# A bidirectional encoder block on one core: split V weights made anew in each group, chunks loaded in place and normalised four at a time, mixed tiles stored from ScalarE's queue

## The chip, the cores and the metric

The kernel runs on one core of a Trainium2 chip. The time is device microseconds of one execution. The kernel before took 1433.19 us, the median of three runs (1433.07, 1433.19, 1435.83). The engines are called TensorE (PE in the profile; PEld is its weight load), VectorE (DVE), ScalarE (ACT), GpSimd (POOL) and SyncE (SP, which here only issues transfers).

## What is computed

One layer on 2048 positions of 1024 features, in float32:

```
h = rms_norm(x, norm_g)
a_val, a_gate, g_conv, u, v, g_sgu = split(h @ w_in, 6)         # each 1024 wide
c = depthwise_conv(a_val * sigmoid(a_gate), width 31) + conv_b
y_conv = silu(layer_norm(c)) * silu(g_conv)
v = layer_norm(v)                                               # over 1024 features
mixed[head] = w_s[head] @ v[chunk of 128 positions, head] + b_s  # 8 heads, 16 chunks
y_sgu = u * mixed * silu(g_sgu)
out = rms_norm(x + concat(y_conv, y_sgu) @ w_out, final_g)
```

## The kernel before

**Numbers.** A float32 product is made of three matmuls in a rounded format: each operand is split into a high and a low part (`split`, L126: ScalarE copies the high part, VectorE subtracts it), and high x high, low x high and high x low are added up in PSUM. So every operand has an "h" and an "l" tile.

**Groups.** The positions are worked on in two groups (g = 0, 1) of two blocks (b = 0, 1) of 512. Each group has a V stage and then 20 units.

*V stage.* `v_mm` (four times 96 matmuls) projects a block onto one half of V's columns. Half 0 of both blocks comes first: `v0_done` takes the statistics of each chunk of 128 positions and stores the chunk to DRAM (`v_sp`). With half 1, `v1_done` (L268 to L281) loads the stored half again (`v0r`, L269), completes the chunk's statistics on VectorE and GpSimd, and normalises both halves on ScalarE (L278, L279) into a place that `room` gives: an r tile, two t tiles, or a w tile. `mix` then multiplies a chunk with the mixing matrices of its heads: two times four small matmuls (L224), a copy by ScalarE (`mixt`, L226) and a store (`mix_sp`, L227). Four chunks are mixed from hooks inside the last `v_mm`, four from the first unit's steps. `make_addend` (g = 0 only) sums the mixing matrices' rows on TensorE (`rsum`) and adds b_s (`bst`).

*The V weights.* `v_weights` (L180) loads them raw in the first group (`vraw`), splits them and stores the split tiles (`op_sp`, from GpSimd's queue, L190 and L191); in the second group it loads the split tiles.

*Sums and units.* `sums_of_a` makes four sums S1 to S4 of the blocks' operands (the `s` tiles, r tiles to s tiles by `split`), one slab of 128 features at a time. A unit makes 2 x 2 blocks of the projection from seven products (`product`, 12 matmuls each, L338) instead of eight, from operands `a` or `s` and weights `op`. The first group builds these weights from raw ones (`w`), a sum and a split each, and stores them to `op_sp`; the second loads them (L298). Some stand in a large tile called `ex`, most in w tiles.

*Conv.* After each conv unit `conv` (44 VectorE instructions) is put in with the lowest priority: a filler. The layer norm of the conv (`conv_ln`) runs later, as a generator in steps, between the output projections (`pa` for the SGU half, `po` for the conv half), which `ln_late` and `ln_first` advance.

**What sets the order.** The code gives each instruction a priority in program order (the conv a low one), and a scheduler at build time picks on each engine among those whose inputs would be there. Every engine then runs its list in that order, and waits at the head of it. Transfers too start in the order of the queue that issues them. A tile waits until its pool has a free buffer: 8 w tiles (512 KB), 3 r tiles (512 KB), 8 t tiles (256 KB), 8 large ones, 6 PSUM banks, and 2 more of these for mixing and small sums.

Of the kernel before, what the change touches and what calls it, by code (L numbers as in the profile page):

```python
# [8 lines left out]
F32 = mybir.dt.float32  # L9
# [5 lines left out]
P = 128  # L15
# [16 lines left out]
def hybrid_block(ctx: ExitStack, tc: tile.TileContext, xt, x, w, wo, wst, vecs, cw, bs, fg, out):  # L32
# [32 lines left out]

    op_sp = dram.tile([156, P, 1024], F32R, name="op_sp")
    v_sp = dram.tile([8, P, SG], F32, name="v_sp")
# [111 lines left out]

    def v_weights(g, half):  # L180
        tiles = []
        for kp in range(4):
            hi, lo = wtile("vh"), wtile("vl")
            at = 140 + half * 8 + kp * 2
            if g == 0:
                r = rtile("vraw")
                for u in range(2):
                    nc.sync.dma_start(r[:, u * 512:(u + 1) * 512], w[2 * half + u, :, kp * 512:(kp + 1) * 512])
# [30 lines left out]
    def mix(ch, zc, wsv):  # L219
        for half in range(2):  # L220
            px = xtile("mixp")
            for h in range(4):
                hd = half * 4 + h
                nc.tensor.matmul(px[:, h * P:(h + 1) * P], zc[half][:, h * P:(h + 1) * P], wsv[half][:, h * P:(h + 1) * P], start=True, stop=True)  # L224
            t = ttile("mixt")
            nc.scalar.activation(t, px, AF.Copy)  # L226
            nc.sync.dma_start(mix_sp[half * 4:half * 4 + 4, :, ch * P:(ch + 1) * P].rearrange("h d s -> d h s"),  # L227
                              t.rearrange("p (h q) -> p h q", h=4))

    def make_addend(wsv):  # L230
        for half in range(2):
            rp = xtile("rsum")
            nc.tensor.matmul(rp, ones, wsv[half], start=True, stop=True)
            bst = ttile("bst")
            nc.sync.dma_start(bst, bs[half * SG:(half + 1) * SG].partition_broadcast(P))
            for h in range(4):
                hd = half * 4 + h
                o = slice(h * P, (h + 1) * P)
                nc.vector.scalar_tensor_tensor(bst[:, o], rp[:, o], sln_b[:, hd:hd + 1], bst[:, o], mul, add)
            nc.sync.dma_start(ad_sp[:, half * 4:half * 4 + 4, :], bst.rearrange("p (h q) -> p h q", h=4))  # L240

    def v_dones(g, wsv):
# [9 lines left out]
        def v0_done_scaled(c, pv):  # L252
# [3 lines left out]
            nc.gpsimd.dma_start(v_sp[c], t)  # L256

        def room(c):
            if c < 3:
                z = rtile("z")  # L260
            elif c == 3:
                return [ttile("z"), ttile("z")]
            else:
                z = wtile("z").bitcast(F32)
            return [z[:, :SG], z[:, SG:]]

        def v1_done(c, pv):
            v0 = ttile("v0r")  # L268
            nc.sync.dma_start(v0, v_sp[c])  # L269
            nc.vector.bn_stats(stats[:, c, 1, :], pv)  # L270
            mv = small.tile([P, 4], F32, tag="mv", name="mv")
            nc.vector.bn_aggr(mv[:, 0:2], stats[:, c].rearrange("p a b -> p (a b)"))
            rs, nm = mv[:, 2:3], mv[:, 3:4]
            nc.gpsimd.tensor_scalar(mv[:, 1:2], mv[:, 1:2], EPS, None, add)
            rsqrt_small(rs, mv[:, 1:2])
            nc.gpsimd.tensor_scalar(nm, mv[:, 0:1], rs, -1.0, mul, mul)
# [8 lines left out]
        return v0_done, v0_done_scaled, v1_done, mix_next  # L285

# [239 lines left out]
    for j in range(2):  # L526
        X[0, j] = btile([P, 2, 4, SG], F32R, f"xg{j}")
    vw = v_weights(0, 0)
    vtiles = None
# [41 lines left out]
    def group(g, A, vtiles):  # L571
        wsv = mixing_weights()
        v0_done, v0_done_scaled, v1_done, mix_next = v_dones(g, wsv)
        if g == 0:
# [9 lines left out]
        v_mm(A, 1, 0, vtiles, v0_done)  # L584
        for t1 in v_weights(g, 1):
# [23 lines left out]
        def build():  # L609
            at = made[0]  # L610
            if at >= len(builders):
                return
            made[0] += 1
            gen, n, j = builders[at]
            if at % 12 < 8:
                t = wtile(f"op{n}_{j}")
            else:
                if ex[0] is None:
                    ex[0] = btile([P, 4, 1024], F32R, "ex")
                t = ex[0][:, at % 12 - 8, :]  # L620
# [11 lines left out]
        for n, (kind, i) in enumerate(units):  # L632
            steps = unit_steps(g, ops, tiles_of.setdefault(n, []), make[kind](i))
            for j in range(6):
                next(steps)
                if n == 0 and j < 4:
                    mix_next()
                    build()
                    if j > 1:
                        build()  # L640
# [16 lines left out]
                if g == 0 and n == NU - 1 and j == 3:  # L657
                    nv = None
                    for nv in v_weights(1, 0):
                        pass  # L660
                    staged_h(nextA, 3, rb[3])
# [88 lines left out]
    for ti in range(HEAD, NT):  # L750
# [16 lines left out]
        ln_first(ti - 12)  # L767

# [18 lines left out]
    for ti in range(NT):  # L787
# [4 lines left out]
        if ti < NT - 1:  # L792
            out_mm(po, yc[ti], 0, (0, 1), False)
            ln_late(ti + 4)
            out_mm(po, yc[ti], 1, (0, 1), True)
            ln_first(ti + 4)
        else:
# [61 lines left out]
```

## Time and profile before

| | |
|---|---|
| median of three runs | 1433.19 us |
| profiled execution, its own time | 1436.89 us |
| its span | 1435.1 us |
| TensorE busy | 1354.6 us, 94% |
| VectorE busy | 1125.2 us, 78% |
| ScalarE busy | 574.7 us, 40% |
| GpSimd busy | 228.9 us, 16% |
| moved by DMA | 341.72 MB, mean 238 GB/s |

All numbers of the trace come from the profiled execution. Busy time counts computing instructions only. The profile also divides the span into 40 slices of 35.9 us; TensorE's busy share in tenths and its granted clock in tenths of full speed read

```profile
PE   6897999999999999947999999999999999999996
PEclk9898999999999999977999999999999999999998
DMA  9326998798989995429877777777588653565641
```

A slice with a 9 is one in which TensorE worked for 90% of the time or more. The low digits lie at the start (first group's V stage), in slices 17 to 19 (second group's V stage and what follows) and at the end.

### The profile page before, as it was taken

To read this page: it belongs to the slowest core of one execution; us is meant where nothing else is said; L and a number is where in the kernel's file an instruction comes from. 1 tells how busy PE (TensorE), PEld (TensorE's weight loads), DVE (VectorE), ACT (ScalarE), POOL (GpSimd) and SP (SyncE) were. 2 spreads that over 40 slices of the span, in tenths; PEclk is the share of its full clock that TensorE was granted. 3 is DMA by queue.
4 is the path that set the end of the run, shared out by engine and by line. 5 is a ranking of instruction groups with operands and counts; after the bars stand their busy time and mean duration, and the time that the engine had idled before them with its cause. 6 is when DMAs were issued, how large, how long until landed. Compare 5 with 4: busy or idle time off the path is not lost. (4 is left out here: it accounts for less than half of the span.)

```text
span 1435.1 us, 17757 instructions
## 1 busy us (share of the span) xinstructions
PE 1354.6 (94%) x6044; PEld 1119.0 (78%) x6044; DVE 1125.2 (78%) x1771; ACT 574.7 (40%) x977; POOL 228.9 (16%) x438
## 2 busy tenths in 40 slices
PE   6897999999999999947999999999999999999996
PEld 5685877888888888836888888888878888788875
DVE  5875578999999999898989999998984112777772
ACT  5444434454445432233222322321244332666662
POOL 1221222333332311131101110110000000011110
PEclk9898999999999999977999999999999999999998
DMA  9326998798989995429877777777588653565641
GB/s 345 130 102 201 342 336 284 261 353 285 320 291 350 330 351 195 158 90 300 283 267 263 260 255 266 272 266 257 195 276 277 185 153 106 183 198 159 191 134 50
DMA packets 169754, 341.72 MB, mean 238 GB/s; under 512 B 15296, under 2 KB 84928, under 8 KB 169664
## 3 DMA queue, kind: packets, MB, share of 16 engines
q1 hardware_dynamic: 135936, 221.04, 47.4%
q0 software_dynamic: 33728, 119.56, 23.0%
q8 instruction: 47, 0.77, 0.2%
q14 instruction: 43, 0.35, 0.1%
HBM read 195.31 MB, written 145.23 MB: 237 GB/s over the span
## 5 line engine op out<-in xcount | busy, mean ns | idle before, releaser
L460 DVE SCALAR_TENSOR_TENSOR ca<-cx,cwt,ca 128x505 f32<-128x505 f32 (+1 forms) x240 | 180.8, 753 | 2.6 <-DMA op<-op_sp 1.4
L462 DVE SCALAR_TENSOR_TENSOR cb<-cx,cwt,cb 128x504 f32<-128x504 f32 (+1 forms) x224 | 168.0, 750 | 4.6 <-ACT cb L456 1.2
L468 DVE SCALAR_TENSOR_TENSOR cb<-cq,cws,cb 128x504 f32<-128x504 f32 (+1 forms) x224 | 168.1, 750 | 0.8
L338 PE MATMUL x<-s,op 128*128 128x512 f32 x648 | 156.2, 389 | 0.0
L338 PEld LDWEIGHTS x<-s,op 128*128 128x128 f32 x648 | 121.5, 188 | 25.1
L204 PE MATMUL v<-vh,a 128*128 128x512 f32 x448 | 123.3, 396 | 4.7 <-ACT a L128 2.4
L204 PEld LDWEIGHTS v<-vh,a 128*128 128x128 f32 x448 | 85.3, 191 | 24.7 <-ACT a L128 4.0
L338 PE MATMUL x<-a,op 128*128 128x512 f32 x336 | 86.7, 396 | 0.0
L338 PE MATMUL v<-a,op 128*128 128x512 f32 x336 | 83.5, 398 | 3.1 <-DVE t L425 3.1
L128 ACT ACTIVATE op<-w 128x512 fp32r<-128x512 f32 x96 | 57.6, 624 | 62.2 <-DVE w L314 41.9
L338 PE MATMUL z<-s,op 128*128 128x512 f32 x336 | 81.4, 391 | 0.0
L338 PE MATMUL y<-a,op 128*128 128x512 f32 x336 | 80.7, 389 | 0.0
L129 DVE TENSOR_TENSOR yl<-ys,yh 128x1024 fp32r<-128x1024 f32 x16 | 19.6, 1224 | 75.5 <-PE pa L684 64.7
L338 PEld LDWEIGHTS v<-a,op 128*128 128x128 f32 x336 | 64.5, 193 | 17.5 <-DVE t L425 3.9
L338 PE MATMUL v<-s,op 128*128 128x512 f32 x312 | 75.3, 390 | 1.6 <-ACT v L418 1.6
L338 PE MATMUL x<-s,ex 128*128 128x512 f32 x312 | 75.3, 389 | 0.0
L311 POOL DMA_DIRECT2D op_sp<-op x96 | 51.4, 535 | 149.6 <-DVE op L129 140.2
L338 PEld LDWEIGHTS x<-a,op 128*128 128x128 f32 x336 | 64.1, 192 | 13.3
L338 PEld LDWEIGHTS z<-s,op 128*128 128x128 f32 x336 | 63.4, 189 | 13.3
L338 PEld LDWEIGHTS y<-a,op 128*128 128x128 f32 x336 | 63.1, 188 | 13.1
L224 PE MATMUL mixp<-wsv,z 128*128 128x128 f32 x256 | 37.3, 305 | 38.1 <-ACT mixt L226 20.0
L129 DVE TENSOR_TENSOR op<-w,op 128x512 fp32r<-128x512 f32 x96 | 64.5, 690 | 10.1 <-ACT op L128 9.8
(167 smaller groups left out, 2714.2 us busy)
## 6 DMA issues: line engine op xcount, KB each, us to landing
op_sp<-op POOLq DMA_DIRECT2D x96, 512.0 KB, 5.7
op<-op_sp SPq DMA_DIRECT2D x96, 512.0 KB, 4.6
op_sp<-ex POOLq DMA_DIRECT2D x44, 512.0 KB, 6.2
ex<-op_sp SPq DMA_DIRECT2D x44, 512.0 KB, 4.5
w<-in_w_dram SPq DMA_DIRECT2D x40, 512.0 KB, 7.0
mix_sp<-mixt SPq DMA_DIRECT2D x32, 256.0 KB, 4.9
glu_sp<-sig POOLq DMA_DIRECT2D x64, 128.0 KB, 4.3
m<-mix_sp SPq DMA_DIRECT2D x32, 256.0 KB, 6.2
```

Source lines behind the costliest of these rows:

```text
L128: nc.scalar.activation(hi, src, AF.Copy)
L129: nc.vector.tensor_tensor(lo, src, hi.bitcast(F32), op=sub)
L204: nc.tensor.matmul(pss[c], A[b, k // 4][:, apart, k % 4, c * P:(c + 1) * P], tiles[k // 2][wpart][:, :, k % 2, :], start=k == 0 and p == 0 ...
L224: nc.tensor.matmul(px[:, h * P:(h + 1) * P], zc[half][:, h * P:(h + 1) * P], wsv[half][:, h * P:(h + 1) * P], start=True, stop=True)
L311: nc.gpsimd.dma_start(op_sp[n * 7 + j], t)
L338: nc.tensor.matmul(acc, tv[:, wpart, kk, :], a[:, apart, kk, :], start=start and p == 0 and kk == 0, stop=p == 2 and kk == 3, skip_group_c ...
L460: stt(a, e[:, j:j + M + 1], cwt[:, i, 2 * j:2 * j + 1], a, mul, add)
L462: stt(b, o[:, j:j + M], cwt[:, i, 2 * j + 1:2 * j + 2], b, mul, add)
L468: stt(b, q[:, j:j + M], cws[:, i, j:j + 1], b, mul, add)
```

## The change

1. `v_weights` loads the raw V weights and splits them in both groups; nothing of them is stored, and `op_sp` is 16 tiles smaller.
2. `room` also loads the stored half of a chunk into its final place. Rooms 0 to 3 are called ahead of the first `v_mm` of half 1, 4 to 7 from hooks in the second. `v1_done` copies the PSUM half beside it, and with every fourth chunk the statistics of four are finished at once (VectorE adds eps and makes -mean x rs, GpSimd one power); ScalarE normalises in place, 1024 columns in one instruction where the place is one tile.
3. The hooks that mix are at k = 3 to 6 (2 to 5 before), the other four chunks in steps 2 to 5 of the first unit (0 to 3 before). Eight operand weights are built ahead of the first unit (four before), and `ex` takes other ones.
4. `mix` stores from ScalarE's queue.
5. `make_addend` loads at a hook in the V stage and does its sums at once.
6. The conv weights are loaded at the very start.
7. The steps of the conv's layer norm come one tile earlier, in both output projections.

```diff
@@ start
+    nc.vector.memset(cwt, 0.0)
+    nc.sync.dma_start(cwt[:, :, 0:TAPS], cw)
     def conv_consts():
-        nc.vector.memset(cwt, 0.0)
-        nc.sync.dma_start(cwt[:, :, 0:TAPS], cw)
@@ v_weights
-            if g == 0:
-                r = rtile("vraw")
-                ...
-                split(hi, lo, r)
-                nc.gpsimd.dma_start(op_sp[at], hi)
-                nc.gpsimd.dma_start(op_sp[at + 1], lo)
-            else:
-                nc.sync.dma_start(hi.bitcast(F32), op_sp[at].bitcast(F32))
-                nc.sync.dma_start(lo.bitcast(F32), op_sp[at + 1].bitcast(F32))
+            r = rtile("vraw")
+            for u in range(2):
+                nc.sync.dma_start(r[:, u * 512:(u + 1) * 512], w[2 * half + u, :, kp * 512:(kp + 1) * 512])
+            split(hi, lo, r)
@@ mix
-            nc.sync.dma_start(mix_sp[...
+            nc.scalar.dma_start(mix_sp[...
@@ v_dones
         def room(c):
-            ...
+            if c == 3:
+                t = [ttile("z"), ttile("z")]
             else:
-                z = wtile("z").bitcast(F32)
-            return [z[:, :SG], z[:, SG:]]
+                z = rtile("z") if c < 4 else wtile("z").bitcast(F32)
+                t = [z[:, :SG], z[:, SG:], z]
+            zs[c] = t
+            nc.sync.dma_start(t[0], v_sp[c])
         def v1_done(c, pv):
-            v0 = ttile("v0r")
-            nc.sync.dma_start(v0, v_sp[c])
+            nc.scalar.activation(zs[c][1], pv, AF.Copy)
             nc.vector.bn_stats(stats[:, c, 1, :], pv)
-            ...
-            zc = room(c)
-            nc.scalar.activation(zc[1], pv, AF.Identity, bias=nm, scale=rs)
-            nc.scalar.activation(zc[0], v0, AF.Identity, bias=nm, scale=rs)
-            pending.append((g * 8 + c, zc, wsv))
+            ...
+            nc.vector.bn_aggr(mv[:, c % 4, 0:2], stats[:, c].rearrange("p a b -> p (a b)"))
+            if c % 4 < 3:
+                return
+            var, rs, nm = mv[:, :, 1], mv[:, :, 2], mv[:, :, 3]
+            nc.vector.tensor_scalar(var, var, EPS, None, add)
+            rsqrt_small(rs, var)
+            nc.vector.scalar_tensor_tensor(nm, mv[:, :, 0], -1.0, rs, mul, mul)
+            for j in range(4):
+                t = zs[c - 3 + j]
+                for z in t[2:] or t:
+                    nc.scalar.activation(z, z, AF.Identity, bias=nm[:, j:j + 1], scale=rs[:, j:j + 1])
+                pending.append((g * 8 + c - 3 + j, t, wsv))
@@ group
+        for c in range(4):
+            room(c)
         ...
-        v_mm(A, 0, 1, t1, v1_done)
+        v_mm(A, 0, 1, t1, v1_done, {2: make_addend(wsv)} if g == 0 else None)
         ...
-        v_mm(A, 1, 1, t1, v1_done, {k: mix_next for k in range(2, 6)})
+        hooks = {k: mix_next for k in range(3, 7)}
+        hooks[1] = lambda: rooms(4, 5)
+        hooks[3] = lambda: (rooms(6, 7), mix_next())
+        v_mm(A, 1, 1, t1, v1_done, hooks)
         if g == 0:
-            make_addend(wsv)
             conv_consts()
...
-        for _ in range(4):
+        for _ in range(8):
             build()
...
-                if n == 0 and j < 4:
+                if n == 0 and j < 2:
+                    continue
+                if n == 0:
                     mix_next()
-                    build()
-                    if j > 1:
+                    if j < 4:
                         build()
                 build()
@@ output projections
-        ln_late(ti - 12)
+        ln_late(ti - 11)
...
-            ln_late(ti + 4)
+            ln_late(ti + 5)
```

What stands on the engines' lists, at three places. SP's list in the second group, from the V stage on (`v0r` or `z` is a stored half of a chunk, `ex` and `op` are unit weights, `wraw` output weights, `cx` the conv's input). Before, from the ex loads on (four v0r loads stand two rows ahead):

```order
L298 DMA ex<-op_sp 128x1024 x4
L227 DMA mix_sp<-mixt 128x4x128 x2
L444 DMA cx<-glu_sp 128x512
L445 DMA cx<-glu_sp 128x512
L227 DMA mix_sp<-mixt 128x4x128
L675 DMA wraw_1_8137<-in_wo_dram 128x1024
L227 DMA mix_sp<-mixt 128x4x128 x2
L675 DMA wraw_2_8141<-in_wo_dram 128x1024
L227 DMA mix_sp<-mixt 128x4x128 x2
L269 DMA v0r<-v_sp 128x512
L227 DMA mix_sp<-mixt 128x4x128
L269 DMA v0r<-v_sp 128x512 x3
```

Now:

```order
L187 DMA vraw<-in_w_dram 128x512 x8
L268 DMA z<-v_sp 128x512 x4
L453 DMA cx<-glu_sp 128x512
L454 DMA cx<-glu_sp 128x512
L268 DMA z<-v_sp 128x512 x4
L307 DMA op_0_5191<-op_sp 128x1024
L307 DMA op_1_5193<-op_sp 128x1024
L694 DMA wraw_0_8071<-in_wo_dram 128x1024
L307 DMA op_2_5195<-op_sp 128x1024
L307 DMA op_3_5197<-op_sp 128x1024
L307 DMA ex<-op_sp 128x1024 x4
```

All eight loads of stored halves have moved ahead of the unit weights, and the mix stores have left the list.

TensorE's list in the second group, from the last matmul of the V stage on (`x`, `y`, `z`, `v` are products of a unit, `s` their sums, `mixp` a half chunk of mixing in each four). Before:

```order
L204 MATMUL v_5044<-vh,a_1_4485 128x512
L224 MATMUL mixp<-wsv,z 128x128 x36
L338 MATMUL x_5257<-a_1_4375,op_0_5249 128x512 x12
L224 MATMUL mixp<-wsv,z 128x128 x4
L338 MATMUL z<-s_1_4812,op_1_5251 128x512 x12
L338 MATMUL x_5257<-s_1_4813,op_2_5253 128x512 x12
L338 MATMUL y<-a_1_4392,op_3_5255 128x512 x12
L224 MATMUL mixp<-wsv,z 128x128 x8
L338 MATMUL v<-s_1_4814,op_4_5288 128x512 x12
L338 MATMUL x_5257<-s_1_4815,op_5_5290 128x512 x6
```

Now:

```order
L198 MATMUL v_5002<-vh,a_1_4446 128x512
L347 MATMUL x_5204<-a_1_4324,op_0_5191 128x512 x12
L347 MATMUL z<-s_1_4794,op_1_5193 128x512 x3
L347 MATMUL x_5204<-s_1_4795,op_2_5195 128x512 x3
L347 MATMUL y<-a_1_4341,op_3_5197 128x512 x12
L347 MATMUL z<-s_1_4794,op_1_5193 128x512 x9
L347 MATMUL x_5204<-s_1_4795,op_2_5195 128x512 x8
L218 MATMUL mixp<-wsv,z 128x128 x4
L347 MATMUL x_5204<-s_1_4795,op_2_5195 128x512
L347 MATMUL x_5368<-a_1_4324,ex 128x512 x12
L218 MATMUL mixp<-wsv,z 128x128 x8
```

Four products, less one matmul, have moved ahead of the mixing that follows the V stage, where 36 matmuls of mixing stood before; the second and the third are each in pieces.

VectorE's list at the start (`xg` is the first operand's low part, `vl` that of the V weights, `cws` sums of conv weights). Before:

```order
L91 MEMSET cwt 128x256
L95 TENSOR_SCALAR vec<-vec 128x8
L536 SCALAR_TENSOR_TENSOR xg_110<-x_108,vec,xg_110 128x512 x2
L129 TENSOR_TENSOR vl<-vraw,vh 128x1024
L536 SCALAR_TENSOR_TENSOR xg_110<-x_108,vec,xg_110 128x512 x2
L129 TENSOR_TENSOR vl<-vraw,vh 128x1024
L536 SCALAR_TENSOR_TENSOR xg_111<-x_108,vec,xg_111 128x512 x2
L129 TENSOR_TENSOR vl<-vraw,vh 128x1024
L94 TENSOR_TENSOR cws<-cwt 128x128
```

Now:

```order
L90 MEMSET cwt 128x256
L96 TENSOR_SCALAR vec<-vec 128x8
L95 TENSOR_TENSOR cws<-cwt 128x128
L545 SCALAR_TENSOR_TENSOR xg_112<-x_110,vec,xg_112 128x512 x2
L130 TENSOR_TENSOR vl<-vraw,vh 128x1024
L545 SCALAR_TENSOR_TENSOR xg_112<-x_110,vec,xg_112 128x512 x2
L130 TENSOR_TENSOR vl<-vraw,vh 128x1024
```

The sum of the conv weights has moved from behind the third V weight to ahead of the first xg instruction.

## Rows read from the trace of the kernel before

**Rows 1.** Stretches of the run: busy time by engine (columns in the first line).
```profile
core 0: us, PE busy (x) PEld busy (x) DVE busy (x) ACT busy (x) POOL busy (x), PEclk, DMA share, GB/s
34.00:52.00 18.00, 9.28 (x23) 5.97 (x24) 14.76 (x30) 8.43 (x15) 4.79 (x6) 0.68 0.30 107
118.00:140.00 22.00, 11.70 (x69) 9.58 (x68) 6.25 (x17) 11.03 (x17) 4.83 (x13) 0.77 0.71 230
140.00:167.00 27.00, 27.00 (x148) 23.35 (x147) 15.74 (x25) 15.55 (x27) 9.05 (x17) 1.00 1.07 357
167.00:200.00 33.00, 28.59 (x112) 22.69 (x112) 18.12 (x29) 12.21 (x23) 9.62 (x18) 0.90 1.00 348
534.00:626.00 92.00, 92.00 (x414) 76.13 (x413) 85.88 (x141) 25.98 (x40) 16.65 (x29) 1.00 0.47 163
626.00:691.00 65.00, 37.21 (x196) 33.15 (x196) 58.56 (x93) 23.48 (x37) 9.80 (x15) 0.76 0.75 250
```

**Rows 2.** Timeline of TensorE, second group: start us, length us, instruction, wait.
```profile
625.62 0.39 PE L204 MATMUL v<-vh,a 128*128 128x512 f32 x1
644.84 7.38 PE L224 MATMUL mixp<-wsv,z 128*128 128x128 f32 x48 [18.82 <-ACT mixt L226]
660.17 3.78 PE L224 MATMUL mixp<-wsv,z 128*128 128x128 f32 x16 [7.95 <-ACT z L279]
666.69 3.93 PE L338 MATMUL x<-a,op 128*128 128x512 f32 x12
688.58 2.88 PE L338 MATMUL x<-a,op 128*128 128x512 f32 x12
```

**Rows 3.** Timeline of VectorE, second group, end of the V stage.
```profile
627.85 1.30 DVE L270 BATCH_NORM_STATS2 stats<-v 128x6 f32<-128x512 f32 x2
647.25 0.72 DVE L129 TENSOR_TENSOR s<-r,s 128x512 fp32r<-128x512 f32 x1
```

**Rows 4.** Timeline of SP's queue, second group.
```profile
656.29 1.97 SPq L269 DMA_DIRECT2D v0r<-v_sp  x3
```

**Rows 5.** Timeline of TensorE, first group.
```profile
117.67 0.39 PE L204 MATMUL v<-vh,a 128*128 128x512 f32 x1
136.14 2.05 PE L224 MATMUL mixp<-wsv,z 128*128 128x128 f32 x8 [10.14 <-DVE bst L239]
152.35 1.95 PE L224 MATMUL mixp<-wsv,z 128*128 128x128 f32 x16
154.05 2.98 PE L338 MATMUL v<-s,op 128*128 128x512 f32 x12
164.11 2.88 PE L338 MATMUL v<-a,op 128*128 128x512 f32 x12
166.83 2.88 PE L338 MATMUL z<-s,ex 128*128 128x512 f32 x12
```

**Rows 6.** Timelines of SP's queue and of VectorE, first group's second unit.
```profile
158.30 1.06 SPq L303 DMA_DIRECT2D w<-in_w_dram  x1
173.78 0.69 DVE L314 TENSOR_TENSOR w<-w,w 128x512 f32<-128x512 f32 x1 [9.27 <-DMA w<-in_w_dram]
```

**Rows 7.** Timelines of ScalarE and TensorE at the start.
```profile
24.70 1.06 ACT L128 ACTIVATE vh<-vraw 128x1024 fp32r<-128x1024 f32 x1 [8.02 <-DMA vraw<-in_w_dram]
39.72 2.06 PE L117 MATMUL rb_x<-dg,ones 128*128 128x512 f32 x2
```

**Rows 8.** Costs by shape (busy, mean ns), and issues (KB, us to landing).
```profile
L278 ACT ACTIVATE z<-v,mv 128x512 f32<-128x512 f32 x16 | 12.4, 778 | 21.4 <-POOL mv L276 21.4
L129 DVE TENSOR_TENSOR vl<-vraw,vh 128x1024 fp32r<-128x1024 f32 x8 | 9.8, 1225 | 1.9 <-ACT vh L128 1.8
op_sp<-vh POOLq DMA_DIRECT2D x8, 512.0 KB, 6.0
cwt<-in_cw_dram SPq DMA_DIRECT2D x1, 124.0 KB, 15.3
```

**Rows 9.** What TensorE waited for: us, times, longest us.
```profile
PE po L684 <- DVE cl L129: 2.3, 3, 0.9
```

More of the change, by code (lines that the diff above doesn't have):

```diff
@@ L64, in xtile @@
         return mx.tile([P, SG], F32, tag="mx", name=name)
-    op_sp = dram.tile([156, P, 1024], F32R, name="op_sp")
+    op_sp = dram.tile([140, P, 1024], F32R, name="op_sp")
     v_sp = dram.tile([8, P, SG], F32, name="v_sp")
@@ L177, in sums_of_a, with v_weights @@
         return sm, part
-    def v_weights(g, half):
+    def v_weights(half):
         tiles = []
@@ L226, in mix, with finish @@
             nc.scalar.activation(t, px, AF.Copy)
-            nc.sync.dma_start(mix_sp[half * 4:half * 4 + 4, :, ch * P:(ch + 1) * P].rearrange("h d s -> d h s"),
+            nc.scalar.dma_start(mix_sp[half * 4:half * 4 + 4, :, ch * P:(ch + 1) * P].rearrange("h d s -> d h s"),
                               t.rearrange("p (h q) -> p h q", h=4))
     def make_addend(wsv):
+        bst = []
         for half in range(2):
[L232 to L240, printed above, removed]
+            bst.append(ttile("bst"))
+            nc.sync.dma_start(bst[half], bs[half * SG:(half + 1) * SG].partition_broadcast(P))
+        def finish():
+            for half in range(2):
+                rp = xtile("rsum")
+                nc.tensor.matmul(rp, ones, wsv[half], start=True, stop=True)
+                for h in range(4):
+                    hd = half * 4 + h
+                    o = slice(h * P, (h + 1) * P)
+                    nc.vector.scalar_tensor_tensor(bst[half][:, o], rp[:, o], sln_b[:, hd:hd + 1], bst[half][:, o], mul, add)
+                nc.sync.dma_start(ad_sp[:, half * 4:half * 4 + 4, :], bst[half].rearrange("p (h q) -> p h q", h=4))
+        return finish
     def v_dones(g, wsv):
@@ L267, in v1_done @@
+        mvs = {}
         def v1_done(c, pv):
-            v0 = ttile("v0r")
-            nc.sync.dma_start(v0, v_sp[c])
+            nc.scalar.activation(zs[c][1], pv, AF.Copy)
             nc.vector.bn_stats(stats[:, c, 1, :], pv)
[L271 to L274, printed above, removed]
@@ L275, in v1_done @@
-            rsqrt_small(rs, mv[:, 1:2])
-            nc.gpsimd.tensor_scalar(nm, mv[:, 0:1], rs, -1.0, mul, mul)
-            zc = room(c)
-            nc.scalar.activation(zc[1], pv, AF.Identity, bias=nm, scale=rs)
-            nc.scalar.activation(zc[0], v0, AF.Identity, bias=nm, scale=rs)
-            pending.append((g * 8 + c, zc, wsv))
+            if c % 4 == 0:
+                mvs[0] = small.tile([P, 4, 4], F32, tag="mv", name="mv")
+            mv = mvs[0]
+            nc.vector.bn_aggr(mv[:, c % 4, 0:2], stats[:, c].rearrange("p a b -> p (a b)"))
@@ L584, in group @@
         v_mm(A, 1, 0, vtiles, v0_done)
-        for t1 in v_weights(g, 1):
+        for t1 in v_weights(1):
             pass
+        for c in range(4):
+            room(c)
         sm, sums = sums_of_a(A, g)
@@ L589, in group, with rooms @@
         sums(1)
-        v_mm(A, 0, 1, t1, v1_done)
+        v_mm(A, 0, 1, t1, v1_done, {2: make_addend(wsv)} if g == 0 else None)
         sums(2)
         sums(3)
-        v_mm(A, 1, 1, t1, v1_done, {k: mix_next for k in range(2, 6)})
+        def rooms(*cs):
+            for c in cs:
+                room(c)
+        hooks = {k: mix_next for k in range(3, 7)}
+        hooks[1] = lambda: rooms(4, 5)
+        hooks[3] = lambda: (rooms(6, 7), mix_next())
+        v_mm(A, 1, 1, t1, v1_done, hooks)
         if g == 0:
-            make_addend(wsv)
             conv_consts()
@@ L614, in build @@
             gen, n, j = builders[at]
-            if at % 12 < 8:
-                t = wtile(f"op{n}_{j}")
-            else:
+            if 4 <= at % 12 < 8:
                 if ex[0] is None:
                     ex[0] = btile([P, 4, 1024], F32R, "ex")
-                t = ex[0][:, at % 12 - 8, :]
+                t = ex[0][:, at % 12 - 4, :]
+            else:
+                t = wtile(f"op{n}_{j}")
             try:
@@ L658, in group @@
                     nv = None
-                    for nv in v_weights(1, 0):
+                    for nv in v_weights(0):
                         pass
```

18 lines of the change are left out of this document (6 added, 12 removed).

## The prediction

> **What bounds the kernel now.** I read the stretches first, then the timelines of the engines that wait in the bad ones. TensorE is full nearly everywhere: from 140 to 167 us and from 534 to 626 us it is busy all the time at a granted clock of 1.00 [rows 1]. So only four stretches have anything to give: the start (34 to 52 us: 8.7 us idle, clock 0.68), the end of the first group's V stage (118 to 140 us: 10.3 idle, 0.77), 167 to 200 us (4.4 idle, 0.90), and the end of the second group's V stage (626 to 691 us: 27.8 idle, 0.76) [rows 1]. A shallow loss at the end, where the output projection waits 2.3 us in all for split conv tiles [rows 9], comes on top.
>
> Second group. The last V matmul starts at 625.62, the first product of the second unit at 688.58 [rows 2]: 62.96 us. The order puts seven chunks of mixing and six products between. A chunk at full clock takes 154.05 - 152.35 = 1.70 us, a product 166.83 - 164.11 = 2.72 us [rows 5], so the work is 7 x 1.70 + 6 x 2.72 = 28.2 us and the loss 34.8 us, in idle time and in work at half clock. Two waits make it: 18.82 us at 644.84 for ScalarE's copy of a mixed tile, and 7.95 us at 660.17 for a normalised chunk [rows 2]. The second is a queue: the last three loads of the stored v0 chunks leave SP only at 656.29 [rows 4], because they stand behind mix stores, ex loads and output weights in that queue. The first is ScalarE's order: mixed copies stand behind the splits of the sums, whose last one leaves VectorE at 647.25, 19.4 us after the statistics at 627.85 [rows 3].
>
> First group. From 117.67 to 166.83 [rows 5] are 49.2 us; seven chunks, eight products and the two row sums (512 columns each, as half a chunk: 0.85) are 11.9 + 21.8 + 1.7 = 35.4, so 13.8 are lost. The one great wait is 10.14 us at 136.14 for the addend's instruction on VectorE [rows 5].
>
> 167 to 200 us is another thing. VectorE waits 9.27 us at 173.78 for a weight whose load had its turn on SP at 158.30, 15.5 us earlier [rows 6], and the DMA share is 1.07 and 1.00 in these two stretches [rows 1]: the transfers are the limit there.
>
> At the start ScalarE waits 8.02 us for raw V weights at 24.70, and the broadcast of the row statistics comes at 39.72 [rows 7].
>
> **The change part by part.** *Early rooms, four chunks normalised at once, mixed stores from ScalarE.* In the second group all eight v0 loads now stand in SP's queue right behind the V weights, ahead of every operand load, and no mix store is in that queue. So the 7.95 us wait goes. The 18.82 us wait goes as well: one chunk is mixed inside the V stage, the next mixing matmul stands behind four products, and no longer 36 in a row ahead of the first. What is late next is the last slab of the sums: on VectorE its first split stands 18 rows behind the last block's first statistics; 32 such rows took 19.4 us [rows 3], so 0.61 each, 11 us. TensorE has 6.8 us of products that don't need it (two whole ones and six matmuls of two others at 0.23), so it waits 4.4 with the copy on ScalarE; then 0.6 for the next split. Four normalisations of 1024 columns stand ahead of mixed copies: between 1.06 us (a plain copy of that width [rows 7]) and 2 x 0.78 (two of 512 [rows 8]); I take 1.24, near the copy, 5 us in all, of which I let 2 show. Work at low clock after the stall: 4, against about 7 now (34.8 - 27.8). Remaining loss 11, **gain 23.8**. Bounds: if nothing goes on before the last split (34 rows, 21 us: 14.2 of wait, 4 of clock, and 6.6 behind norms and copies) 10; if only 2 are lost, 33.
>
> In the first group the addend's loads are issued in the V stage and its two row sums run there, and the v0 loads no longer stand behind mix stores. So the 10.14 us wait goes. Late next: the three r tiles hold chunks until they are mixed, and the first unit's weights need r tiles, so its second weight load comes only behind the second mix; and the fourth mix waits for copies behind the normalisations. I leave 5 of 13.8, **gain 8.8**; bounds 3 and 12.
>
> ScalarE's issues: three issues took SP 1.97 us [rows 4], 0.66 each; 32 are 21 us of ScalarE, which is busy 26 of 92 us in a full stretch [rows 1]. Only those of the V stages lie beside copies that TensorE waits for: **cost 2**, between 0 and 6 (nine of them bare).
>
> *V weights split anew.* In the second group eight subtractions of 1.225 us [rows 8], 9.8 us of VectorE, and eight copies of 1.06 us [rows 7] on ScalarE are added, at the end of the first group and through the second's V stage. VectorE is busy 85.88 of 92 us there [rows 1], but with the conv's instructions, which have the lowest priority and go elsewhere: cost 0, 9.8 if that cover is gone. In the first group 16 stores of 512 KB (6.0 us to landing [rows 8]) go. Half of them belong to the first V weights and lie beside the loads of raw weights and x. Without them the 8.02 us wait [rows 7] shrinks by some 6.
>
> *Conv weights first.* Their 124 KB took 15.3 us to landing [rows 8], while issued among big loads and stores; now they are third on SP, and VectorE's sum over them stands ahead of its first xg instruction. I take 1.5 us of delay, because only x stands ahead of them in the queue and no stores run. With that and a shorter stay at clock 0.68 (1.0) the start gives 6 - 1.5 + 1.0 = **5.5**; bounds: 9 gained (the wait and the clock whole), 3 lost (all 15.3 us kept, most of it hidden under the 8.02 us wait and the squares behind it).
>
> *167 to 200 us.* The loads of the second block's v0 (4 x 256 KB) leave the crowded time, 3 us of DMA, and 118 to 140 had 0.29 of 22 us free [rows 1], 6.4 us. So the engines can follow some 9.4 us of advance, about what the first group gains, and no more: **0** here, between -8.8 (the gain given back) and +7.7 (4.4 idle and 0.10 of 33 us of clock).
>
> *Norm of the conv one tile earlier.* Of the 2.3 us [rows 9] I take **1.0**; bounds 0 and 2.3.
>
> Sum: 23.8 + 8.8 + 5.5 + 0 + 1.0 - 2 = 37.1. The profiled execution took 1436.89, so 1399.8; it lies 3.7 above the median of the runs shown, 1433.19, so **1396**.
>
> **The rivals.**
> *B, VectorE's sums still set the second group.* The last split is as far behind the V stage as before (34 rows for 32), and there are 9.8 us of new subtractions. If products and mixing wait for it, that group gains 10: 1396 + 13.8 = 1410. Against it: four products precede the first mixing now.
> *F, the DMA engines set the first group.* Shares of 1.07 and 1.00 for 60 us [rows 1] speak for it: what TensorE gains before 167 it waits for later. 1396 + 8.8 = 1405. The Trainium skill, DMA: Bandwidth & Descriptors, section Issuing engines are not separate DMA queues, says that transfers started from different engines share the same 16 DMA engines, and that only issue time is saved; by that rule ScalarE's queue moves no byte sooner here, and F's time would hold. The trace of before has the shares, but no store from ScalarE.
> *E, the conv weights hold up the start.* 124 KB in 15.3 us [rows 8] is 8 GB/s; if that is their own pace, xg and the first weight come late and the start loses 3: 1396 + 8.5 = 1404 or 1405. Against it: the raw weights issued behind them landed by 24.70 [rows 7], so that the 15.3 us may be those of the whole crowd. The same page's section Specifications wants 512 bytes or more in a transfer for full rate; a row of 31 floats has 124, so by that rule E would be the case. Small transfers are in the trace only with others around.
> *C, nearly all stalls go.* The good ends together: 32 + 12 + 9 + 4 + 2 = 59, less issue at 0 and 1 more from clock: 1433.19 - 60 = 1373. Against it: the split 11 us behind V.
> *D, slower.* A store on ScalarE's queue holds the copies behind it: it waits for its own mixed tile and for its issue. From 0.66 us to about 2.1 per store, 1.5 more x 32 = 48: 1396 + 48 = 1444. It decides from 37.1 / 32 = 1.2 us more per store. For it: each copy frees one of two buffers that the next mixing needs. Against it: SP spent 0.66 per issue, and half of the stores lie where ScalarE has time.
>
> **How the numbers follow.** A 0.47 (own range 1386 to 1405), B 0.17, F 0.13, C 0.09, E 0.08, D 0.06. The range runs from 1377, which leaves half of C out, to 1414, which leaves out D and B together with F. About 0.2%, 2.9 us, is what a measurement can tell from no change. Everything but D is faster by more: faster 0.92, same 0.02 (where several bad ends meet), slower 0.06.
>
> **What would show it.** Right: no wait above 6 us on TensorE between the second V stage and its second unit, and about 39 us between them for 63; in the first group about 40 for 49; the row statistics' broadcast near 35. Wrong: a wait for the split of the sums of over 10 us (B); more idle time than 4.4 us behind the first group's second unit, with DMA full (F); the first weights waiting for the conv weights' sum on VectorE and the broadcast past 40 (E); TensorE waiting for ScalarE's copies of mixed tiles or units while ScalarE idles between its own stores (D).

## The result, and the profile after

The kernel after takes 1381.46 us (median of four runs, 1378.5 to 1384.35), the one before 1433.13 on the same chip: a ratio of 0.9636, interval 0.9612 to 0.9659. A second measurement on another chip gave 0.9629 (0.9611 to 0.9647). That is 52 us less. The forecast was 37 (1396, range 1377 to 1414).

The span of the profiled execution fell from 1435.1 to 1376.7 us, by 58.4. The profiled execution before lay 3.7 above its median and this one 3.0 below its own, so the profiles show some 7 us more than the medians. The stretches after, columns as in [rows 1]:

```profile
core 0: us, PE busy (x) PEld busy (x) DVE busy (x) ACT busy (x) POOL busy (x), PEclk, DMA share, GB/s
34.00:52.00 18.00, 14.64 (x54) 10.42 (x53) 15.66 (x29) 9.05 (x16) 3.40 (x5) 0.81 0.16 59
118.00:140.00 22.00, 20.94 (x118) 17.92 (x117) 11.39 (x18) 16.13 (x26) 5.07 (x10) 1.00 0.91 299
140.00:167.00 27.00, 27.00 (x137) 22.95 (x136) 14.67 (x23) 11.67 (x21) 9.43 (x18) 1.00 1.10 367
167.00:200.00 33.00, 33.00 (x147) 27.34 (x146) 30.07 (x48) 16.11 (x26) 8.51 (x16) 1.00 1.04 369
500.00:560.00 60.00, 58.64 (x257) 47.75 (x256) 58.48 (x87) 23.50 (x33) 5.41 (x10) 1.00 0.55 188
600.00:626.00 26.00, 23.09 (x115) 18.22 (x114) 26.00 (x48) 11.99 (x19) 1.38 (x1) 1.00 0.83 286
626.00:691.00 65.00, 64.23 (x324) 54.29 (x323) 59.70 (x89) 21.73 (x34) 6.78 (x16) 1.00 0.92 316
```

Behind the second V stage, now at 600 us, TensorE is idle for 2.9 of 26 us, and its clock never leaves 1.00; before it was idle for 27.8 of 65, at 0.76 [rows 1]. The stretch from 167 to 200 us is full, at a DMA share no lower than before. The same places on TensorE (start us, length, instruction, wait), second group and then first:

```profile
599.90 0.39 PE L198 MATMUL v<-vh,a 128*128 128x512 f32 x1
605.44 3.03 PE L347 MATMUL y<-a,op 128*128 128x512 f32 x12 [0.80 <-DMA op<-op_sp]
613.19 2.11 PE L347 MATMUL x<-s,op 128*128 128x512 f32 x8 [1.42 <-ACT s L129]
653.56 0.62 PE L347 MATMUL x<-a,op 128*128 128x512 f32 x2
111.78 0.39 PE L198 MATMUL v<-vh,a 128*128 128x512 f32 x1
122.27 2.15 PE L218 MATMUL mixp<-wsv,z 128*128 128x128 f32 x16 [1.06 <-ACT mixt L220]
150.70 0.61 PE L347 MATMUL x<-s,op 128*128 128x512 f32 x2
```

The last V matmuls stand at 599.90 and 111.78, before at 625.62 and 117.67 [rows 2, 5]. Up to 653.56 the second group has done seven chunks of mixing and 13 products, 47.3 us by the prices of [rows 5], in 53.7: a loss of 6.4 for the 34.8 of before. Up to 150.70 the first has done seven chunks and nine products, 36.4 in 38.9: 2.5 for 13.8. The waits of 18.82, 7.95 and 10.14 us [rows 2, 5] are gone; the longest that is left here is 1.42.

The start, on three engines (VectorE's first sum of conv weights, ScalarE's fourth V weight, TensorE's broadcast), two issues of mix stores, the commonest and the longest, and the landing of the conv weights (KB, us):

```profile
6.57 0.29 DVE L95 TENSOR_TENSOR cws<-cwt 128x128 f32<-128x128 f32 x1 [3.94 <-DMA cwt<-in_cw_dram]
16.29 1.06 ACT L129 ACTIVATE vh<-vraw 128x1024 fp32r<-128x1024 f32 x1
35.36 1.10 PE L118 MATMUL rb_x<-dg,ones 128*128 128x512 f32 x2
613.65 0.37 ACTq L221 DMA_DIRECT2D mix_sp<-mixt  x1
145.67 3.91 ACTq L221 DMA_DIRECT2D mix_sp<-mixt  x1
cwt<-in_cw_dram SPq DMA_DIRECT2D x1, 124.0 KB, 4.8
```

The fourth V weight is split at 16.29 for 24.70, without a wait, and the broadcast comes at 35.36 for 39.72 [rows 7]. The conv weights landed 4.8 us after their issue, for 15.3 [rows 8]. The start is not full even so: behind the broadcast TensorE waits 3.36 us for an operand split on ScalarE, and from 34 to 52 us it is busy for 14.64 of 18 us at 0.81.

### The profile page after: what moved, and what is told of

It reads as the page before. It is cut to its first block, busy times and chain, and to the rows that moved or that the text cites. A ratio compares the mean times of both kernels' runs of the same rounds, so it can differ in the third digit from the quotient of the medians.

```text
span 1376.7 us, 17691 instructions
## 1 busy us (share of the span) xinstructions
PE 1342.3 (97%) x6044; PEld 1108.7 (81%) x6044; DVE 1134.8 (82%) x1787; ACT 584.8 (42%) x987; POOL 198.0 (14%) x378
## 4 chain that ended last, share of the span: by engine, by line
PE 73%; DVE 11%; issue 9%; DMA 4%; POOL 1%; ACT 1%; SPq 0%; POOLq 0%; DVEq 0%; ACTq 0%
PE x L347 17%; PE pa L703 13%; PE po L703 12%; PE v L347 11%; PE v L198 7%; PE y L347 6%; PE z L347 5%; DVE ca L469 2%; DVE cb L477 2%; PE mixp L218 1%; DVE cb L471 1%; DMA xrow<-in_x_dram 1%; DVE op L130 1%; DMA mix_sp<-mixt 1%; DMA op_sp<-ex 1%
## 5 line engine op out<-in xcount | busy, mean ns | idle before, releaser
L347 PEld LDWEIGHTS x<-s,op 128*128 128x128 f32 x624 | 116.8, 188 | 26.2 <-ACT s L129 1.7
L347 PE MATMUL x<-s,ex 128*128 128x512 f32 x336 | 81.4, 390 | 0.0
L347 PE MATMUL x<-a,op 128*128 128x512 f32 x312 | 79.1, 391 | 0.0
L347 PE MATMUL v<-a,op 128*128 128x512 f32 x312 | 75.1, 390 | 0.1
L347 PEld LDWEIGHTS x<-s,ex 128*128 128x128 f32 x336 | 62.9, 188 | 12.9
L198 PE MATMUL v<-vl,a 128*128 128x512 f32 x224 | 68.5, 394 | 1.0 <-DVE vl L130 1.0
L347 PEld LDWEIGHTS y<-a,op 128*128 128x128 f32 x312 | 58.4, 188 | 13.7 <-DMA op<-op_sp 1.2
L418 ACT ACTIVATE y<-x 128x512 f32<-128x512 f32 x40 | 23.3, 582 | 108.3 <-PE x L347 108.3
L347 PEld LDWEIGHTS v<-a,op 128*128 128x128 f32 x312 | 58.5, 188 | 12.7 <-DVE t L434 0.5
L347 PEld LDWEIGHTS x<-a,op 128*128 128x128 f32 x312 | 58.5, 188 | 12.5 <-issue 0.5
```

What stands on the lines that cost most here:

```text
L198: nc.tensor.matmul(pss[c], A[b, k // 4][:, apart, k % 4, c * P:(c + 1) * P], tiles[k // 2][wpart][:, :, k % 2, :], start=k == 0 and p == 0 ...
L347: nc.tensor.matmul(acc, tv[:, wpart, kk, :], a[:, apart, kk, :], start=start and p == 0 and kk == 0, stop=p == 2 and kk == 3, skip_group_c ...
L418: nc.scalar.activation(y, x0, AF.Copy)
```

## The experiments

Ratios are to the kernel before on the same chip; the kernel after is 0.9636 and 0.9629, and "worse by" is against 0.9632 of 1433 us.

**1. One part taken back from the kernel after.**

*Mix stores on SP again.*
```diff
-            nc.scalar.dma_start(mix_sp[half * 4 ...
+            nc.sync.dma_start(mix_sp[half * 4 ...
```


> The kernel after, with the mix stores issued from SP again. Theory Q (queue): in the kernel before the third unit's second weight load stood behind four mix stores on SP that waited for mixed tiles; without stores in that queue the load leaves early, and this is where the 8 to 10 us of the first group's second and third unit went that the prediction had put at 0. Then this kernel loses 8 to 15 us (1390 to 1396) and VectorE waits again for a weight load between 150 and 190 us. Rival E (early chunks): all loads come early because the chunks are ready early, whatever queue stores them; then 1380 to 1384 and no such wait. Prediction's own rival D, that stores on ScalarE cost, would make it faster, below 1379.

Measured 0.9682 (0.9650 to 0.9714), worse by 7 us. That lies between Q's 8 to 15 and E's 3 at the most, and the interval touches both; the wait that Q forecast and E ruled out is there. Rival D is out. The profiled execution is the slowest of its four (1392.74, median 1384.9), so its span is no measure. VectorE does wait for a weight again; SP's queue, then VectorE:

```profile
145.80 8.80 SPq L221 DMA_DIRECT2D mix_sp<-mixt  x4
157.81 0.34 SPq L312 DMA_DIRECT2D w<-in_w_dram  x1
173.90 1.29 DVE L323 TENSOR_TENSOR w<-w,w 128x512 f32<-128x512 f32 x2 [8.01 <-DMA w<-in_w_dram]
```

But the load did not leave late, as Q had it. It left at 157.81, in the kernel after at 159.25. It landed late: 16.1 us after its issue, for 9.5 here in the kernel after:

```profile
159.25 0.33 SPq L312 DMA_DIRECT2D w<-in_w_dram  x1
168.76 1.29 DVE L323 TENSOR_TENSOR w<-w,w 128x512 f32<-128x512 f32 x2 [0.22 <-DMA w<-in_w_dram]
```

*V weights stored and loaded again* (the old `v_weights`).
```diff
+            if g == 0:
...
+                nc.gpsimd.dma_start(op_sp[at], hi)
+                nc.gpsimd.dma_start(op_sp[at + 1], lo)
+            else:
+                nc.sync.dma_start(hi.bitcast(F32), op_sp[at].bitcast(F32))
+                nc.sync.dma_start(lo.bitcast(F32), op_sp[at + 1].bitcast(F32))
```


> The kernel after, with the split V weights stored in the first group and loaded in the second, as before. Theory S (stores crowd the start): the raw weights' wait at the start comes back, the broadcast of the row statistics moves from 35.4 to 38 to 40 us, and the whole loses 3 to 6 us (1384 to 1388); the second group gains nothing from eight subtractions less on VectorE. Rival V: VectorE's 9.8 us in the second group cost about 2 us (units 200 to 534 us lost 2.3 in the kernel after), so this kernel gains that back and loses less than 2 in all, 1379 to 1383.

Measured 0.9752 (0.9724 to 0.9780), worse by 17 us. S had the start right (the broadcast at 40.11) and the whole far too small; V is wrong. The profiled execution is the slowest of its four and lies 22 us behind the profile of the kernel after. TensorE's longest waits in it behind the one for its first weights (us in total, times, longest):

```profile
PE z L354 <- ACT s L129: 7.4, 1, 7.4
PE x L354 <- ACT op L129: 4.4, 1, 4.4
PE pc L124 <- DVE ss L563: 3.8, 1, 3.8
```

The 3.8 is the start, the 4.4 stands in the first group at 133 us, and the 7.4 in the second group. There VectorE's list came out otherwise: from the last block's first statistics to the first split of the last slab it is 21.7 us here, and 9.1 in the kernel after (601.39 to 610.53).

```profile
605.47 0.70 DVE L281 BATCH_NORM_STATS2 stats<-v 128x6 f32<-128x512 f32 x1
627.20 0.70 DVE L130 TENSOR_TENSOR s<-r,s 128x512 fp32r<-128x512 f32 x1
```

*Conv weights loaded late.*
```diff
     def conv_consts():
+        nc.vector.memset(cwt, 0.0)
+        nc.sync.dma_start(cwt[:, :, 0:TAPS], cw)
```


> The kernel after, with the conv weights loaded where they were before. They landed in 4.9 us when third in the queue, for 15.3 in the crowd, so theory: no change, 1380 to 1383, and the load takes 5 to 9 us to land in its old place since there are no V weight stores beside it now. Rival: their place at the head delays the first weights by some us; then this kernel starts earlier (first product before 9.0 us, for 9.64) and gains 1 to 3, 1378 to 1380.

Measured 0.9630 (0.9607 to 0.9653): no change, as expected. The load lands in 7.2 us in its old place, so it was the crowd that made 15.3. The first product stands at 8.91 for 9.64, as the rival here had it, but the kernel after run a second time has it at 10.97, and the time shows no gain. Rival E of the prediction is out.

*Norm steps at their old tiles.*
```diff
-        ln_late(ti - 11)
+        ln_late(ti - 12)
...
-            ln_late(ti + 5)
+            ln_late(ti + 4)
```


> The kernel after, with the conv's layer norm steps at their old tiles. The last 250 us gained about 4 us where the prediction had 1. Theory L: the earlier steps gave it; this kernel loses 3 to 4 (1384 to 1386), and the output projections wait over 2 us more for split conv tiles. Rival: the gain comes from elsewhere (the conv's end, other buffers' turns), and this kernel is within 1 us of the one after.

Measured 0.9655 (0.9631 to 0.9678), worse by 3 us, but the intervals overlap, and the waits for split conv tiles are 2.3 us for 1.4, not 2 more. Theory L fits the size and not the place. Counted by TensorE's matmuls, its profile lies 4.9 us behind that of the kernel after: 3.2 of them are lost between the 2000th and the 2200th, where the second group begins, and 2.0 from the 4200th to the end. So the steps can be worth some 2 us, and that is not clear of the noise.

*Chunks loaded and normalised one at a time.*
```diff
         def v1_done(c, pv):
-            nc.scalar.activation(zs[c][1], pv, AF.Copy)
+            v0 = ttile("v0r")
+            nc.sync.dma_start(v0, v_sp[c])
...
+            zc = room(c)
+            nc.scalar.activation(zc[1], pv, AF.Identity, bias=nm, scale=rs)
+            nc.scalar.activation(zc[0], v0, AF.Identity, bias=nm, scale=rs)
```


> The kernel after, with chunks loaded and normalised one at a time as before (load, statistics on GpSimd, two normalisations of 512 columns), all else as after. Theory B: the early load and the joint normalisation carry most of the first and second group's gain; this kernel loses 15 to 30 us, 1396 to 1411, and TensorE waits again over 5 us for a normalised chunk. Rival Q: with mix stores gone from SP and mixing later, the chunks are in time either way; it loses under 6, below 1387.

Measured 0.9847 (0.9816 to 0.9878), worse by 31 us: theory B, at the upper edge of its range. TensorE waits again for a mixed tile in the second group, 13.41 us at 622 (18.82 before), and for a normalised chunk: 7.42 us at 125, in the first group, and 4.96 in the second (7.95 before):

```profile
622.11 8.47 PE L218 MATMUL mixp<-wsv,z 128*128 128x128 f32 x48 [13.41 <-ACT mixt L220]
125.25 3.78 PE L218 MATMUL mixp<-wsv,z 128*128 128x128 f32 x16 [7.42 <-ACT z L279]
635.54 3.78 PE L218 MATMUL mixp<-wsv,z 128*128 128x128 f32 x16 [4.96 <-ACT z L279]
```

*Mixing steps, early builds and ex as before; and, in another kernel, the addend behind the V stage as before.*
```diff
-        for _ in range(8):
+        for _ in range(4):
             build()
-                if n == 0 and j < 2:
-                    continue
-                if n == 0:
+                if n == 0 and j < 4:
                     mix_next()
```
```diff
-        v_mm(A, 0, 1, t1, v1_done, {2: make_addend(wsv)} if g == 0 else None)
+        v_mm(A, 0, 1, t1, v1_done)
...
         if g == 0:
+            make_addend(wsv)
```


> The kernel after, with the four late mixes in steps 0 to 3 of the first unit, four weight builds ahead of it and ex for the same weights as before. Theory H: mixing then stands on TensorE's list ahead of the products again and waits for ScalarE behind the splits of the sums; it loses 8 to 20 us, mostly in the second group (1389 to 1401). Rival B: chunks are normalised early enough, and it loses under 4 us.

> The kernel after, with the addend made behind the V stage as before. Theory: its 10.14 us wait in the first group comes back in part, 5 to 9 us, 1386 to 1390, and no other stretch changes. Rival: the loads for it now leave SP without mix stores ahead of them, and TensorE has products to do, so it costs under 2 us.

Measured 0.9749 (0.9717 to 0.9782) and 0.9730 (0.9701 to 0.9758), worse by 17 and 14 us. The size is H's in the first and beyond the range in the second, but the places are mostly wrong in both. The addend's wait in the first group does not come back. Against the profile of the kernel after, the first kernel loses 10 us and the second 8 from the 2000th to the 2600th matmul, around the place where the second group begins; 4 us of the first come behind the second V stage, where H had put them. In the second kernel, two waits of TensorE, and what SP's loads of raw V weights waited for (us in total, times, longest):

```profile
518.81 1.94 PE L198 MATMUL v<-vh,a 128*128 128x512 f32 x4 [4.35 <-ACT vh L129]
521.94 1.65 PE L198 MATMUL v<-vl,a 128*128 128x512 f32 x3 [1.20 <-DVE vl L130]
SPq L187 <- DVE a L130: 8.1, 3, 5.9
```

Those are the addend kernel's first V matmuls of the second group. Its raw V weights pass the three r tiles, behind x and the last unit's weights: from 485 to 530 us their loads stand on SP for 8.1 us until VectorE has split operands made from x, 8.7 in the kernel with the old mixing steps, and 1.7 in the kernel after.

**2. One part alone, put into the kernel before.**

*Mix stores from ScalarE's queue.*
```diff
-            nc.sync.dma_start(mix_sp[half * 4 ...
+            nc.scalar.dma_start(mix_sp[half * 4 ...
```


> The kernel before, with only the mix stores moved to ScalarE's queue. Theory Q (SP's queue was what held late loads): the v0 loads of the second group leave early, its 7.95 us wait goes, and the weight wait at 173.78 shrinks, together 10 to 16 us: ratio to before 0.989 to 0.993. Rival B (the normalising one chunk at a time sets these stretches, whatever queue stores): within 3 us of before, ratio 0.998 to 1.002. Rival D (stores on ScalarE hold its copies): slower than before.

Measured 0.9936 (0.9915 to 0.9958), 9 us faster; D is out again. The ratio is just above Q's range, whose edge lies in the interval, and Q is right in one place of two: the stretch from 167 to 200 us is full, and from the 600th to the 800th matmul this kernel gains 7.9 us on the one before; but the waits of the second group stay (18.5 and 5.5 us). The third unit's load left at 157.37, 0.9 us earlier than before [rows 6], and landed within 8.8:

```profile
157.37 0.33 SPq L303 DMA_DIRECT2D w<-in_w_dram  x1
166.20 1.29 DVE L314 TENSOR_TENSOR w<-w,w 128x512 f32<-128x512 f32 x2 [0.25 <-DMA w<-in_w_dram]
140.00:167.00 27.00, 27.00 (x145) 23.26 (x144) 15.51 (x25) 14.68 (x26) 9.30 (x18) 1.00 1.08 366
```

*Early rooms and joint normalisation* (the new `v_dones`; mixing still from k = 2 and in steps 0 to 3).
```diff
+        for c in range(4):
+            room(c)
...
-        v_mm(A, 1, 1, t1, v1_done, {k: mix_next for k in range(2, 6)})
+        hooks = {k: mix_next for k in range(2, 6)}
+        hooks[1] = lambda: rooms(4, 5)
+        hooks[3] = lambda: (rooms(6, 7), mix_next())
+        v_mm(A, 1, 1, t1, v1_done, hooks)
```


> The kernel before, with the early load, the place of each chunk and the joint normalisation of the kernel after, all else as before (mix stores on SP, mixing in steps 0 to 3 and from k = 2, V weights stored, addend behind the V stage). Theory B (this part carries the gain of both V stages): since the kernel after lost 30 us without it, it alone gains 20 to 30 us, ratio 0.979 to 0.986. Rival T (the parts need each other: with mixing still ahead of the products on TensorE's list, it waits for the copies behind the sums' splits as before): it gains under 12 us, ratio above 0.9915, and the wait of 18 us for a mixed tile stays in the second group.

Measured 0.9825 (0.9810 to 0.9839), 25 us faster: theory B. The wait of 18 us is gone and T is out: with the chunks early, the scheduler put the mixing behind the unit's first products by itself, though the code asks for it at the first step. In its profile this kernel is 30 us ahead of the one before at the end of the second V stage and its first units, some 26 of them won there. Ahead of that it won 1 us in the first group's V stage, 10 right behind it, where the wait of 10.14 us for the addend is gone though the addend's code stayed, and 8 more up to the 1000th matmul. It lost 15 again in the first group's later units, where TensorE waits for VectorE, six times in the whole run. The waits for mixed tiles are the second line:

```profile
PE v L347 <- DVE t L434: 9.7, 6, 4.0
PE mixp L224 <- ACT mixt L226: 3.6, 4, 1.7
```

*V weights split anew.*
```diff
-            if g == 0:
-                r = rtile("vraw")
...
-                nc.gpsimd.dma_start(op_sp[at], hi)
+            r = rtile("vraw")
...
+            split(hi, lo, r)
```


> The kernel before, with V weights split anew in each group. Storing them again in the kernel after cost 16 us: 4 at the start, 4 in the first group's weights, 8 in the second group, where the sums' last slab came later on VectorE's list. Theory L (only the start is the part's own, the rest is how the list fell out): alone it gains 3 to 5 us at the start, loses 1 to 6 at the second group's first V matmuls, which wait for raw weights through the r tiles, and ends between 0.996 and 1.002. Rival S (splitting anew helps the second group itself): it gains over 8 us, ratio below 0.994, with a shorter wait behind the second V stage.

Measured 0.9906 (0.9888 to 0.9923), 13 us faster: L is too low; S has the size right, and the wait behind the second V stage is shorter, as it said (13.22 us for 18.82). By the profile the start and first V stage gain 8 of them, 7 the stretch up to 200 us, 6 the second group (the profiled execution is the fastest of its kernel, 4.5 us below the median). Here too the third unit's load stood behind four mix stores, and took 16.8 us:

```profile
139.75 8.71 SPq L220 DMA_DIRECT2D mix_sp<-mixt  x4
148.91 1.02 SPq L296 DMA_DIRECT2D w<-in_w_dram  x1
165.69 1.29 DVE L307 TENSOR_TENSOR w<-w,w 128x512 f32<-128x512 f32 x2 [9.65 <-DMA w<-in_w_dram]
```

**3. The price at the second group's start.** The kernel with the late addend, and half 0 of the V weights stored split.
```diff
+            if g == 0 or half == 1:
...
+                if half == 0:
+                    nc.gpsimd.dma_start(op_sp[at], hi)
+                    nc.gpsimd.dma_start(op_sp[at + 1], lo)
+            else:
+                nc.sync.dma_start(hi.bitcast(F32), op_sp[at].bitcast(F32))
```


> The kernel after with the addend made late (which lost 13 us, 7 of them where the second group begins and its first V matmuls wait for weights split from raw ones), and besides with half 0 of the V weights stored split in the first group and loaded in the second. Theory R (raw V weights have to pass the three r tiles behind x and the last unit's weights): the waits for vh and vl at the second group's start go, TensorE is full from 500 to 560 us, 5 to 8 us come back there, and the start loses the 4 us that the stores cost; in all 2 to 4 us faster than with the addend late alone (ratio 0.970 to 0.972). Rival: the loss there has another cause (the last units' weights), and the waits go but the time at the 2300th matmul stays as late as with the addend late alone.

Measured 0.9755 (0.9738 to 0.9772), where the late addend alone had 0.9730 (0.9701 to 0.9758): the intervals overlap, and the 2 to 4 us that were expected as a gain did not come. R is right on the waits for vh and vl: gone. But only some 4 us came back there, as much as this kernel had lost ahead of it, most of that in the first V stage, where the stores are. The reason is that the operands made from x, which pass the same r tiles, are late next (1.21 and 2.56 us). The 2300th matmul stands at 541.06 us for 540.90, which is the sign that the rival named; its cause, the last units' weights, was not tried. Behind the second V stage TensorE waits 5.48 us for a split sum whose copy stood behind four normalisations on ScalarE:

```profile
524.27 1.20 PE L206 MATMUL v<-vh,a 128*128 128x512 f32 x4 [1.21 <-ACT a L129]
528.94 3.43 PE L206 MATMUL v<-vh,a 128*128 128x512 f32 x8 [2.56 <-DVE a L130]
624.86 4.64 ACT L290 ACTIVATE z<-z,mv 128x1024 f32<-128x1024 f32 x4 [1.41 <-DVE mv L286]
630.07 3.78 PE L349 MATMUL x<-s,op 128*128 128x512 f32 x8 [5.48 <-ACT s L129]
```

*The kernel after again, as a yardstick.*

> The kernel after itself, beside the others on the same chip, as their yardstick: ratio 0.961 to 0.966 to the kernel before.

Measured 0.9629, as told above.

## Why the prediction was right, and where its terms were off

The direction, the places and the main mechanism were right; the sum was too small, 37 us for 52. By step, in the profiled executions (the rest of their 58.4 us, some 2, was not followed):

| step | forecast | measured |
|---|---|---|
| second group, V stage to units | 23.8 | 28.4 (34.8 - 6.4) |
| first group, V stage to units | 8.8 | 11.3 (13.8 - 2.5) |
| start and first V stage | 5.5 | 5.9 (117.67 - 111.78) |
| 167 to 200 us | 0 | 7.7 |
| mix stores issued by ScalarE | -2 | 0 to -1 (waits for mixed tiles 1.8, and 0.9 with the stores on SP) |
| V weights anew, second group's start | 0 | -1.4 (500 to 560 us) |
| tail, from the 4200th matmul on | 1.0 | 4.3, some 2 of them with the norm steps, the rest open |

*The step that failed* is "167 to 200 us ... the transfers are the limit there". A DMA share near 1 was read as a limit on all transfers alike. The load that VectorE waited for took 15.5 us [rows 6] behind four mix stores on the same queue, 16.1 and 16.8 in two other kernels with four stores just ahead of it, and 8.8 and 9.5 in two with those stores on ScalarE's queue, at shares of 1.07, 1.11, 1.05, 1.08 and 1.10 and 357 to 377 GB/s from 140 to 167 us. With two stores ahead (early rooms alone) it took 11.8. What changed is how much SP's queue had to move. From the load's issue to its landing (packets, MB, share of 16 engines), in the kernel before (158.30 to 173.78), and then with only the mix stores moved (157.37 to 166.20); q0 is GpSimd's queue, q1 SP's, q10 ScalarE's:

```profile
q0 software_dynamic: 1066, 3.81, 69.2%
q1 hardware_dynamic: 1700, 1.72, 38.2%
q0 software_dynamic: 556, 2.02, 62.2%
q10 hardware_dynamic: 1066, 0.53, 24.2%
q1 hardware_dynamic: 199, 0.75, 22.6%
```

SP's queue moved 1.72 MB until this load of 0.52 MB had landed, and 0.75 without the stores; in the other two slow cases it was 1.76 and 1.90, in the other fast one 0.89. Its pace was 85 to 113 GB/s in all five, so the load was late for what its queue carried with it, while GpSimd's queue had 62 to 74% of the engines' time. So rival F fell with the rule that it leaned on: the section of the Trainium skill cited there (DMA: Bandwidth & Descriptors, Issuing engines are not separate DMA queues) says that starting transfers from several engines saves issue time alone, and here it set the landing of a load on the other queue; the measurement decides. How the DMA engines take turns between queues is not shown. Nor is this the only way out of that stall: split V weights or early chunks alone gained there as well, where the same load left at 148.91 and 151.18 and not at 158.30 [rows 6].

*Second group.* The mechanism is as told: the split stood 9.1 us behind the statistics, 11 forecast, and four products covered it. Three sizes were off. TensorE's waits for these splits came to 2.1 us and not 5.0. "Work at low clock after the stall: 4" did not come: the granted clock stayed at 1.00, and the longest wait left is 1.42 us. And the normalisations of 1024 columns (1.24 us, as taken) let nothing show where 2 were put, since the copy that TensorE waited for stood ahead of them on ScalarE; where it stood behind them, in the kernel with half 0 stored, 5.48 us showed. The part behind it was known right: early rooms and joint normalising alone give 25 us, and the kernel after without them loses 31.

*V weights.* The cover of VectorE's eight subtractions held (the longest wait for one is 1.03 us), and the stores' crowd at the start was worth what was forecast. Missed was the other side: raw weights need r tiles, and the second group's first matmuls wait for them. In the kernel after that costs 1.4 us; with slightly other lists it was 8 to 10 more. And when the weights were stored again, 5.7 of the 22 us by which that profile lies behind are lost in the start and first V stage, where the stores are; some 8 came with another order on VectorE's list, and what made the 4.4 us wait was not followed.

*Parts do not add up.* Taken back one by one, the parts cost 7, 17, 0, 3, 31, 17 and 14 us, 89 in all for a change of 52. Each edit makes the scheduler write other lists, so an undone part carries the price of a new order too; no run here separates the two.

## What to carry to other kernels

A wait for a load in a time of full DMA engines is to be read with its queue: add up what that queue has to move until the load has landed, and not the bytes of all queues together. Here stores that nobody waited for soon did better on another queue than the loads that somebody did. Work that ends one stage and is needed in the next is best brought forward in all its inputs: here a chunk's place, its load and its statistics together took it off TensorE's path. Where a scheduler writes the lists, the gain of one part is measured by adding it and by taking it away, and the two numbers differ: here 9 and 7 us for the queue of the mix stores, 25 and 31 for the early chunks, 13 and 17 for the V weights.

## What was not expected of the hardware

Issuing a store from ScalarE took 0.37 to 0.46 us in 28 of 32 cases and 0.77 to 3.91 in four, all between 126 and 155 us, where the DMA share is 1.09: 18.4 us in all on a ScalarE that is 42% busy, near the 21 us of the prediction's price. TensorE's waits for mixed tiles are still only 1.8 us in all. And a 124 KB load of 124-byte rows landed in 15.3, 7.2 and 4.8 us at three times with the same rows, so what ran beside it made most of the 15.3. The least of these, 26 GB/s, is far below the 367 GB/s of the busy stretch, so they do not speak against the line of the Trainium skill (DMA: Bandwidth & Descriptors, Specifications) that rival E named, 512 bytes or more for full rate; what the row length costs by itself no run here shows.
